# Activations and weight rings of the feed-forward stages placed above 128 KB of each partition

## The chip, the cores and the metric

The kernel runs as one program on one core of a Trainium2 chip. The measure is the time that the device takes for one execution, in microseconds (us), as the median of several runs. TensorE (PE) multiplies matrices and loads the stationary operand (PEld); VectorE (DVE), ScalarE (ACT) and GpSimd (POOL) do elementwise work; SyncE (SP) issues the DMA transfers of weights. Operands lie in SBUF, which has 128 partitions; an address here is the place of a tile within its partition, in KB from its start, and a tile has the same place in each.

## What is computed

A model of two blocks on 256 tokens of width 1024, in float32. The first block (attention, memory attention and a mixture of experts) takes the first 1187 us of the profiled span. The change lies in the second block:

```python
def swiglu(h, w_in, w_out):
    gate, up = jnp.split(h @ w_in, 2, axis=-1)
...
    for l in range(DEPTH):                      # DEPTH = 2
        h = rms_norm(x, norm_ffa[l])
        x = x + 0.5 * swiglu(h, ffa_w_in[l], ffa_w_out[l])
...
        x = x + hybrid_mixer(h, w_in[l], ...)
        h = rms_norm(x, norm_ffb[l])
        x = x + 0.5 * swiglu(h, ffb_w_in[l], ffb_w_out[l])
    return rms_norm(x, norm_final)
```

So there are four feed-forward stages, called here FFN a and FFN b of layers 0 and 1, and a mixer between a and b of each layer. The hidden width of a feed-forward is 2816.

## The kernel before

A float32 operand is split into two float32r parts, hi and lo, and `mm3` (L93) adds three products: hi by hi, lo by hi and hi by lo. A product is one matmul of 128x256 with a weight load of 128 columns.

A feed-forward (`ffn`, L345) runs over 11 chunks of 256 hidden columns. Each chunk has 48 gate products, 48 up products (both against the normed input) and 48 down products (against the activations), 1584 for the stage. The weights of each are one [128, 8, 256] block, which `chunk` (L213) loads in two halves of 512 KB: half i goes through ring i of `e.rings`, a list of three pools each. The load lands in tile `w`; ACT casts it into `whi` (L229); DVE takes the difference into `wlo` (L231). Before, ring 0 is `e.w2`, which lives through the whole block and is the mixers' only ring, and ring 1 (`fw`, `fwhl`, `fwlo`) is opened by `scopes` for the feed-forward.

The normed input is written by `gain_h` (L301): for each of eight row tiles ACT writes `hh` (L308) and DVE `hl` (L309). The sum of squares for the norm is taken beside it (L283 on ACT, two TENSOR_REDUCEs of L284 on DVE, a RECIPROCAL, L290, after a square root on ACT, L289) and applied to the products. `split_act` writes the activations' parts `ah` and `al` (L316, L317) for the down products. A mixer ends with the products of `y` (tiles `y4`) by `w_out`, whose results are added into `xT` (L1031); the next `hh` is read from there.

A scheduler lays out each engine's instructions in one order, in which the engine then works through them; a tile whose place is still read by earlier work can only be written when that work is done. Places follow from the order in which pools are opened. The tiles of the built programs lie as follows (KB; "mod" is the address by 512 bytes):

```
                          before                    after
hh, hl                    26.9, 34.9  mod 416       FFN a l0: 136.2, 144.2  mod 224
                                                    FFN b l0, FFN a l1: 135.2, 143.2  mod 224
                                                    FFN b l1: 135.4, 143.4  mod 416
                                                    mixers: 58.9, 66.9  mod 416
ah, al                    106.9 to 114.9  mod 416   127.2 to 136.2  mod 224
w2 ring (w / whi / wlo)   42.9 / 54.9 / 66.9        26.9 / 38.9 / 50.9  mod 416 both
ring 1 before             74.9 / 86.9 / 94.9        -
ring fa, FFN a l0         -                         81.2 / 93.2 / 105.2  mod 224
rings fa, fb, later       -                         151.2 to 215.4  mod 224 (FFN b l1: mod 416)
first chunk's weights     192.0 to 208.0  mod 480   the same (FFN a l0 only)
y4 of the mixers          129.7 to 165.7  mod 224   the same
block 1: P, nhl (L1790)   172 to 181, 192 to 207, equal mod 512
block 1: hh, weights      208, 130 to 144, differing by 64 mod 512
```

Of the kernel before, what the change touches and what calls it, by code (L numbers as in the profile page):

```python
# [11 lines left out]
F32 = mybir.dt.float32  # L12
# [8 lines left out]
T = 256  # L21
D = 1024
# [19 lines left out]
def constant_tables():  # L42
    """Tables that follow from the shapes alone, laid out by partition."""
# [51 lines left out]
def mm3(nc, out, L, R, first, last, skip=False):  # L95
    """out += L^T R for float32 operands held as two float32r parts each."""
# [7 lines left out]
def bc(ap, axis, n):  # L104
    """Insert a broadcast axis of size n at position axis."""
    shape = list(ap.shape)
    idx = [slice(None)] * axis + [None] + [slice(None)] * (len(shape) - axis)
    shape.insert(axis, n)
    return ap[tuple(idx)].to_broadcast(shape)
# [37 lines left out]
def constants2(e):  # L147
    """The loads of the mixers' constants, and what follows from them."""
# [16 lines left out]
def scopes(e, kind):  # L165
    e.stack = ExitStack()
    P = lambda n, b: e.stack.enter_context(e.tc.tile_pool(name=n, bufs=b, reuse_waits="tile"))
    if kind == "ffn":
        banks(e, bank=4, sbank=2, ubank=2)
        e.rings = [e.w2, [P("fw", 3), P("fwhl", 2), P("fwlo", 3)]]  # L170
        e.act = P("fact", 2)
        e.s1 = P("fs1", 6)
        e.s2 = P("fs2", 4)
        e.s4 = P("fs4", 2)
    elif kind == "mix":
        banks(e, bank=3, abank=3, sbank=2)
        e.rings = [e.w2]
        e.act = P("act", 2)
# [12 lines left out]

def banks(e, **n):
    """The scope's PSUM banks, by ring."""
# [10 lines left out]
def hcol(e, l, name, i):  # L204
    """Half of the vector: a sigmoid is 0.5 tanh(x / 2) + 0.5."""
# [4 lines left out]
def ccol(e, l, name, i):  # L210
    """1 less the vector, or less its half."""
# [4 lines left out]
def chunk(e, src, after=()):  # L216
    """A [128, a, 2048 / a] block of weights; (hi, lo) float32r parts of each of its a row tiles. The lo queue
    behind after."""
# [19 lines left out]
def behind(e, tail):  # L238
    """A block whose instructions are queued behind those of tail, each on its engine."""
# [14 lines left out]
def proj_T(e, u, h, c0=0, bank=None):  # L254
    """One bank [feature, 2, token]: columns c0.. of the chunk's row tiles against h."""
# [9 lines left out]
def proj_N(e, u, h):  # L265
    """One bank [token, 2, column]."""
# [9 lines left out]
def rms_row(e, cols=False, bank=None):  # L276
    """1 / rms of each token, on every partition; with cols also by token on the partitions."""
# [23 lines left out]
def gain_h(e, l, name):  # L301
    """x^T times the norm's gain, split in two parts; 1 / rms is applied to the products."""
    nc = e.nc
    hh = e.per.tile([128, KD, T], F32R, name="hh")
    hl = e.per.tile([128, KD, T], F32R, name="hl")
# [15 lines left out]
def warm(e, fn, after):  # L321
    """Loads an activation's table, behind after."""
# [4 lines left out]
def ffn(e, l, name, wi, wo):  # L327
    nc = e.nc
    if name == "norm_ffa" and l == 0 or name == "norm_ffb":
        scopes(e, "ffn")  # L330
# [16 lines left out]
    for c in range(nc2):  # L347
        u, e.first = e.first, None
# [28 lines left out]
def rope(e, x, cos, sin, half):  # L377
    """In-place rotation of the first 2*half entries of the last axis; x [128, 2, heads, dim]."""
# [1734 lines left out]
```

## Time and profile before

| | |
|---|---|
| three runs | 2719.51, 2721.08, 2724.07 us; median 2721.08 us |
| span of the profiled execution | 2723.9 us, 2.8 us above that median |
| PE busy | 2623.9 us, 96% |
| DVE, ACT busy | 1371.4 us (50%), 1011.8 us (37%) |
| DMA | mean 254 GB/s over the span |

The profile is of one execution; its busy times are those of records on each engine. In the span, FFN a of layer 0 runs from about 1187 to 1380 us, the mixer to 1764, FFN b to 1950; layer 1's FFN a to 2143, its mixer to 2522, its FFN b to 2716.

### The profile page before, as it was taken

To read this page: it belongs to the slowest core of one execution; us is meant where nothing else is said; L and a number is where in the kernel's file an instruction comes from. 1 tells how busy PE (TensorE), PEld (TensorE's weight loads), DVE (VectorE), ACT (ScalarE), POOL (GpSimd) and SP (SyncE) were. 2 spreads that over 40 slices of the span, in tenths; PEclk is the share of its full clock that TensorE was granted. 3 is DMA by queue.
4 is the path that set the end of the run, shared out by engine and by line. 5 is a ranking of instruction groups with operands and counts; after the bars stand their busy time and mean duration, and the time that the engine had idled before them with its cause. 6 is when DMAs were issued, how large, how long until landed. Compare 5 with 4: busy or idle time off the path is not lost.

```text
span 2723.9 us, 43485 instructions
## 1 busy us (share of the span) xinstructions
PE 2623.9 (96%) x17866; PEld 1993.2 (73%) x17866; DVE 1371.4 (50%) x2204; ACT 1011.8 (37%) x1662; POOL 107.1 (4%) x171
## 2 busy tenths in 40 slices
PE   8999998999999998999999999999999999999998
PEld 8643332448543333369999988999999999889998
DVE  6521100027421000055577887765755678977655
ACT  7311000027211000044466554544444565645543
POOL 0000000000000000000000031000000000320000
PEclk9999999999999999999999999999999999999999
DMA  9899999996899999985655533656566555426653
GB/s 348 317 372 409 409 409 377 406 379 218 321 358 409 409 409 384 409 281 180 186 155 153 161 102 101 213 179 186 178 184 182 154 165 157 132 86 189 194 178 116
DMA packets 353715, 691.64 MB, mean 254 GB/s; under 512 B 25872, under 2 KB 229648, under 8 KB 352992
## 3 DMA queue, kind: packets, MB, share of 16 engines
q1 hardware_dynamic: 351488, 681.38, 71.4%
q0 software_dynamic: 976, 5.70, 0.5%
q8 instruction: 145, 2.38, 0.4%
q10 hardware_dynamic: 1040, 1.64, 0.2%
q14 instruction: 66, 0.54, 0.1%
HBM read 684.47 MB, written 4.19 MB: 253 GB/s over the span
## 4 chain that ended last, share of the span: by engine, by line
PE 50%; DMA 5%; DVE 5%; ACT 1%; issue 1%; SPq 0%; DVEq 0%; ACTq 0%
PE sbank L100 23%; PE ubank L100 9%; PE bank L100 9%; PE bank L1843 2%; DVE wlo L231 2%; DMA w<-in_w_up_dram 1%; PE abank L100 1%; DVE t L796 1%; DMA w<-in_w_down_dram 1%; DMA w<-in_w_gate_dram 1%; DMA w<-in_ffb_w_in_dram 1%; PE bank L899 1%; ACT whi L229 0%; DMA w<-in_w_out_dram 0%; DVE t L797 0%
## 5 line engine op out<-in xcount | busy, mean ns | idle before, releaser
L229 ACT CAST whi<-w 128x1024 fp32r<-128x1024 f32 x452 | 471.1, 1049 | 538.5 <-PE sbank L100 249.8
L231 DVE TENSOR_TENSOR wlo<-w,whi 128x1024 fp32r<-128x1024 f32 x452 | 550.3, 1222 | 126.4 <-PE sbank L100 51.7
L1843 PE MATMUL bank<-w,xg 128*64 128x512 f32 x1960 | 492.6, 598 | 24.6 <-DMA w<-in_w_up_dram 21.4
L1843 PEld LDWEIGHTS bank<-w,xg 128*64 128x64 f32 x1960 | 163.7, 136 | 340.3 <-issue 262.3
L100 PE MATMUL sbank<-hh,whi 128*128 128x256 f32 x1408 | 404.8, 288 | 6.5 <-ACT whi L316 6.0
L100 PE MATMUL sbank<-hh,wlo 128*128 128x256 f32 x1408 | 404.0, 287 | 6.1 <-DVE wlo L231 6.0
L100 PE MATMUL sbank<-hl,whi 128*128 128x256 f32 x1408 | 402.6, 286 | 1.0 <-DVE hl L309 0.9
L100 PEld LDWEIGHTS sbank<-hh,whi 128*128 128x128 f32 x1408 | 271.3, 193 | 10.2 <-ACT whi L316 6.6
L100 PEld LDWEIGHTS sbank<-hh,wlo 128*128 128x128 f32 x1408 | 270.9, 193 | 10.2 <-DVE wlo L231 7.0
L100 PEld LDWEIGHTS sbank<-hl,whi 128*128 128x128 f32 x1408 | 271.1, 193 | 4.2 <-issue 2.2
L1843 PE MATMUL bank<-w,aT 128*64 128x512 f32 x1024 | 249.6, 604 | 18.8 <-PEq L1936 12.7
L1843 PEld LDWEIGHTS bank<-w,aT 128*64 128x64 f32 x1024 | 86.3, 138 | 169.1 <-issue 147.9
L100 PE MATMUL ubank<-hh,wlo 128*128 128x256 f32 x704 | 199.4, 283 | 0.0
L100 PE MATMUL ubank<-hh,whi 128*128 128x256 f32 x704 | 199.3, 283 | 0.0
L100 PE MATMUL ubank<-hl,whi 128*128 128x256 f32 x704 | 199.2, 283 | 0.0
L100 PE MATMUL bank<-al,whi 128*128 128x256 f32 x704 | 194.1, 283 | 1.0 <-DVE al L317 1.0
L100 PE MATMUL bank<-ah,wlo 128*128 128x256 f32 x704 | 194.3, 283 | 0.0
L100 PE MATMUL sbank<-wlo,hh 128*128 128x256 f32 x624 | 181.6, 291 | 1.4 <-DVE wlo L231 0.7
L100 PE MATMUL bank<-ah,whi 128*128 128x256 f32 x704 | 179.0, 283 | 0.2 <-ACT ah L316 0.2
L100 PE MATMUL sbank<-whi,hh 128*128 128x256 f32 x624 | 178.4, 287 | 0.0
L100 PE MATMUL sbank<-whi,hl 128*128 128x256 f32 x624 | 178.2, 286 | 0.0
L1910 DVE TENSOR_TENSOR xn<-fbank,xn 128x512 f32<-128x512 f32 x60 | 41.5, 691 | 261.6 <-PE fbank L1908 261.6
(510 smaller groups left out, 4233.6 us busy)
## 6 DMA issues: line engine op xcount, KB each, us to landing
w<-in_w_gate_dram SPq DMA_DIRECT2D x128, 1024.0 KB, 18.4
w<-in_w_down_dram SPq DMA_DIRECT2D x124, 1024.0 KB, 18.4
w<-in_w_up_dram SPq DMA_DIRECT2D x117, 1024.0 KB, 18.4
w<-in_w_in_dram SPq DMA_DIRECT2D x140, 512.0 KB, 3.7
w<-in_ffa_w_in_dram SPq DMA_DIRECT2D x88, 512.0 KB, 4.7
w<-in_ffb_w_in_dram SPq DMA_DIRECT2D x88, 512.0 KB, 4.6
w<-in_ffa_w_out_dram SPq DMA_DIRECT2D x44, 512.0 KB, 4.2
w<-in_ffb_w_out_dram SPq DMA_DIRECT2D x44, 512.0 KB, 4.2
```

The source lines that it names most:

```text
L100: m = nc.tensor.matmul(out, a, b, start=first and i == 0, stop=last and i == 2, skip_group_check=skip)
L229: c = nc.scalar.copy(hi, w)
L231: m = nc.vector.tensor_sub(lo, w, hi.bitcast(F32))
L796: nc.vector.tensor_mul(tmp, X[:, :, :t + 1], bc(LXv[:, :t + 1, t], 1, 16))
L899: nc.tensor.matmul(py[t][32 * c:32 * c + 32, P], RpT[t][:, P, 32 * c:32 * c + 32], cur[:, P], start=True, stop=True, tile_position=(0, 32 ...
L1843: m = nc.tensor.matmul(pb[n][64 * i:64 * i + 64], lhs(k, i), ws[i][j][:, sl], start=k == 0, stop=k == KD - 1, tile_position=(0, 64 * i))
L1910: nc.vector.tensor_add(yacc[t][:, sl], out, yacc[t][:, sl])
```

## The change

`scopes` opens the pools of a feed-forward in another order. In FFN a of layer 0 (where `e.first` is set) the rings stay low, and 15 KB of empty room put the activations and `hh`, `hl` above 128 KB. In the other feed-forwards 46 KB (layer 0) or 34 KB (layer 1) of empty room stand below the activations, `hh`, `hl`, and two rings, `fa` and `fb`, and chunk 0 still takes its first halves through `w2`; from chunk 1 on both halves go through `fa` and `fb`. The mixers get a pool for `hh`, `hl` of their own. Elsewhere the file only loses its docstrings, so line numbers are shifted by up to 20 (L231 is L249, L309 is L327).

```diff
-def scopes(e, kind):
+def scopes(e, kind, l=0):
...
         banks(e, bank=4, sbank=2, ubank=2)
-        e.rings = [e.w2, [P("fw", 3), P("fwhl", 2), P("fwlo", 3)]]
-        e.act = P("fact", 2)
         e.s1 = P("fs1", 6)
         e.s2 = P("fs2", 4)
         e.s4 = P("fs4", 2)
+        ring = lambda n, h=3: [P("w" + n, 3), P("h" + n, h), P("l" + n, 5 - h)]
+        if e.first:
+            a = ring("fa")
+            space(P, 15)
+            e.act = P("fact", 2)
+            e.hp = P("hp", 1)
+            e.steady = [e.w2, a]
+        else:
+            space(P, 46 - 12 * l)
+            e.act = P("fact", 2)
+            e.hp = P("hp", 1)
+            a = ring("fa")
+            e.steady = [a, ring("fb", 2)]
+        e.rings = [e.w2, a]
     elif kind == "mix":
         banks(e, bank=3, abank=3, sbank=2)
         e.rings = [e.w2]
+        e.hp = P("hp", 1)
...
+def space(P, kb):
+
+    P("space", 1).tile([128, 256 * kb], F32, name="space")
...
-    hh = e.per.tile([128, KD, T], F32R, name="hh")
-    hl = e.per.tile([128, KD, T], F32R, name="hl")
+    hh = e.hp.tile([128, KD, T], F32R, name="hh")
+    hl = e.hp.tile([128, KD, T], F32R, name="hl")
...
-        scopes(e, "ffn")
+        scopes(e, "ffn", l)
...
     for c in range(nc2):
+        if c == 1:
+            e.rings = e.steady
...
-    yo = [e.act.tile([128, D], F32, name="yo", bufs=2) for _ in range(2)]
-    z = [e.act.tile([128, 512], F32, name="z", bufs=2) for _ in range(2)]
+    yo = [e.s1.tile([128, D], F32, name="yo", bufs=2) for _ in range(2)]
+    z = [e.s1.tile([128, 512], F32, name="z", bufs=2) for _ in range(2)]
```

The scheduler's order moves with it. On DVE, at the end of layer 0's mixer and the start of FFN b, the program before has these rows (xT of L1031 are the mixer's last additions; wlo of L231 stand for weights of the mixer, then of FFN b; four of the eight hl stand ahead of them):

```order
L1031 TENSOR_TENSOR xT<-sbank,xT 128x512
L231 TENSOR_TENSOR wlo<-w,whi 128x1024 [waits DMAHW2_49,Activation_49]
L231 TENSOR_TENSOR wlo<-w,whi 128x1024 [waits DVE_49,DMAHW4_49,PE_49,Activation_49]
L309 SCALAR_TENSOR_TENSOR hl<-xT,vec,hh 128x256 [waits Activation_49] x2
L231 TENSOR_TENSOR wlo<-w,whi 128x1024 [waits DMAHW5_49,PE_49,Activation_49]
L1031 TENSOR_TENSOR xT<-sbank,xT 128x512
L284 TENSOR_REDUCE t_14650<-t_14652 128x256 [waits Activation_49]
L231 TENSOR_TENSOR wlo<-w,whi 128x1024 [waits DMAHW6_49,DVE_49,PE_49]
L309 SCALAR_TENSOR_TENSOR hl<-xT,vec,hh 128x256 [waits Activation_49] x2
L284 TENSOR_REDUCE t_14651<-t_14655 128x256 [waits Activation_49]
L231 TENSOR_TENSOR wlo<-w,whi 128x1024 [waits DMAHW1_49,PE_49,Activation_49]
L285 TENSOR_TENSOR t_14649<-t_14650,t_14651 128x256 [waits DVE_49]
```

And the changed program these, from the wlo that waits for the mixer's last product on (the second row is the last xT; the wlo are, in turn, those of up's first half, gate's second half, down, up's second half, two of other loads, and after the RECIPROCAL chunk 1's gate):

```order
L249 TENSOR_TENSOR wlo<-w,whi 128x1024 [waits DVE_49,DMAHW7_49,PE_49,Activation_49]
L1051 TENSOR_TENSOR xT<-sbank,xT 128x512
L327 SCALAR_TENSOR_TENSOR hl<-xT,vec,hh 128x256 [waits Activation_49] x8
L302 TENSOR_REDUCE t_14680<-t_14684 128x256 [waits Activation_49]
L249 TENSOR_TENSOR wlo<-w,whi 128x1024 [waits DMAHW2_49,Activation_49,Pool_49]
L249 TENSOR_TENSOR wlo<-w,whi 128x1024 [waits DMAHW0_49,PE_49]
L303 TENSOR_TENSOR t_14678<-t_14679,t_14680 128x256 [waits DVE_49]
L249 TENSOR_TENSOR wlo<-w,whi 128x1024 [waits DMAHW3_49,Activation_49]
L249 TENSOR_TENSOR wlo<-w,whi 128x1024 [waits DMAHW1_49,PE_49,Activation_49]
L249 TENSOR_TENSOR wlo<-w,whi 128x1024 [waits DMAHW4_49,DVE_49,PE_49]
L308 RECIPROCAL t_14690<-t_14690 128x256 [waits Activation_49]
L249 TENSOR_TENSOR wlo<-w,whi 128x1024 [waits DMAHW6_49,DVE_49,PE_49]
```

All eight hl now stand in one piece behind the last xT, the second TENSOR_REDUCE behind them, and the wlo of the chunk's second halves behind that.

On ACT at the same place the program before has (casts of L229 are of weights, hh of L308; four more hh stand ahead):

```order
L229 CAST whi<-w 128x1024 [waits DMAHW1_49]
L229 CAST whi<-w 128x1024 [waits DMAHW2_49,Pool_49]
L229 CAST whi<-w 128x1024 [waits DMAHW4_49,PE_49,Activation_49]
L308 ACTIVATE hh<-xT,vec 128x256 [waits DVE_49]
L308 ACTIVATE hh<-xT,vec 128x256
L229 CAST whi<-w 128x1024 [waits DMAHW5_49,PE_49,Activation_49]
L229 CAST whi<-w 128x1024 [waits DMAHW6_49,PE_49,Activation_49]
L283 ACTIVATE t_14652<-xT 128x1024
L308 ACTIVATE hh<-xT,vec 128x256 [waits DVE_49]
L308 ACTIVATE hh<-xT,vec 128x256
L283 ACTIVATE t_14655<-xT 128x1024
L229 CAST whi<-w 128x1024 [waits DMAHW1_49,PE_49,Activation_49]
```

and the changed program (casts are L247 there, hh is L326), whose second row is the cast that waits for the last but one product of the mixer:

```order
L247 CAST whi<-w 128x1024 [waits DMAHW7_49,DVE_49,PE_49]
L247 CAST whi<-w 128x1024 [waits DMAHW0_49,DVE_49,PE_49]
L326 ACTIVATE hh<-xT,vec 128x256 x4
L326 ACTIVATE hh<-xT,vec 128x256 [waits DVE_49]
L326 ACTIVATE hh<-xT,vec 128x256
L326 ACTIVATE hh<-xT,vec 128x256 [waits DVE_49]
L326 ACTIVATE hh<-xT,vec 128x256
L301 ACTIVATE t_14684<-xT 128x1024
L247 CAST whi<-w 128x1024 [waits DMAHW2_49]
L247 CAST whi<-w 128x1024 [waits DMAHW3_49,Pool_49]
L247 CAST whi<-w 128x1024 [waits DMAHW4_49]
L247 CAST whi<-w 128x1024 [waits DMAHW1_49,PE_49,Activation_49]
```

All eight hh have moved behind the mixer's products.

On DVE at the start of FFN a of layer 0 the program before has, left out between its second and third row some constants and two wlo:

```order
L309 SCALAR_TENSOR_TENSOR hl<-xT,vec,hh 128x256 [waits DMAHW4_49,DMAHW5_49,DMAHW0_49,Activation_49]
L309 SCALAR_TENSOR_TENSOR hl<-xT,vec,hh 128x256 [waits Activation_49] x7
L231 TENSOR_TENSOR wlo<-w,whi 128x1024 [waits DMAHW3_49,Activation_49]
L231 TENSOR_TENSOR wlo<-w,whi 128x1024 [waits DMAHW5_49,Activation_49]
L284 TENSOR_REDUCE t_7741<-t_7743 128x256 [waits Activation_49]
L284 TENSOR_REDUCE t_7742<-t_7746 128x256 [waits Activation_49]
L231 TENSOR_TENSOR wlo<-w,whi 128x1024 [waits DMAHW4_49,DVE_49,PE_49]
L285 TENSOR_TENSOR t_7740<-t_7741,t_7742 128x256 [waits DVE_49]
```

and the changed program, left out in the same way behind the first four rows:

```order
L327 SCALAR_TENSOR_TENSOR hl<-xT,vec,hh 128x256 [waits DMAHW2_49,DMAHW1_49,DMAHW3_49,DMAHW0_49,Activation_49]
L327 SCALAR_TENSOR_TENSOR hl<-xT,vec,hh 128x256 [waits Activation_49] x3
L302 TENSOR_REDUCE t_7748<-t_7750 128x256 [waits DMAHW3_49,DMAHW4_49,DMAHW2_49,Activation_49]
L327 SCALAR_TENSOR_TENSOR hl<-xT,vec,hh 128x256 [waits Activation_49] x4
L249 TENSOR_TENSOR wlo<-w,whi 128x1024 [waits DMAHW5_49,Activation_49]
L249 TENSOR_TENSOR wlo<-w,whi 128x1024 [waits DMAHW4_49,DVE_49,PE_49]
L302 TENSOR_REDUCE t_7749<-t_7753 128x256 [waits Activation_49]
L303 TENSOR_TENSOR t_7747<-t_7748,t_7749 128x256 [waits DVE_49]
L249 TENSOR_TENSOR wlo<-w,whi 128x1024 [waits DMAHW6_49,PE_49]
```

One of the two TENSOR_REDUCEs has moved between the hl, and a wlo that stood behind both now stands ahead of the other.

## Rows read from the trace of the kernel before

**Rows 1.** the page, sections 1 and 2: TensorE's row and its granted clock

```profile
PE 2623.9 (96%) x17866; PEld 1993.2 (73%) x17866; DVE 1371.4 (50%) x2204; ACT 1011.8 (37%) x1662; POOL 107.1 (4%) x171
...
PEclk9999999999999999999999999999999999999999
```

**Rows 2.** windows in the feed-forward: busy us, PEclk, DMA share, GB/s

```profile
1780.00:1950.00 170.00, 169.80 (x1415) 169.60 (x1415) 99.18 (x103) 74.20 (x83) 0.00 (x0) 1.00 0.60 180
1970.00:2140.00 170.00, 170.00 (x1419) 170.00 (x1418) 99.62 (x103) 75.02 (x83) 0.00 (x0) 1.00 0.59 177
```

**Rows 3.** the timeline in FFN b, layer 0, first and last of 28

```profile
1903.78 0.28 PE L100 MATMUL sbank<-hh,wlo 128*128 128x256 f32 x1
...
1907.02 0.28 PE L100 MATMUL ubank<-hl,whi 128*128 128x256 f32 x1
```

**Rows 4.** the timeline in FFN a, layer 0, chunk 0, 28 products

```profile
1194.79 0.28 PE L100 MATMUL sbank<-hh,whi 128*128 128x256 f32 x1
...
1197.97 0.28 PE L100 MATMUL sbank<-hh,whi 128*128 128x256 f32 x1
```

**Rows 5.** the timeline in block 1, first and last of 49

```profile
20.13 0.28 PE L100 MATMUL sbank<-hh,whi 128*128 128x256 f32 x1
...
25.57 0.28 PE L100 MATMUL sbank<-whi,hh 128*128 128x256 f32 x1
```

**Rows 6.** instructions of line 1790: minimum, median, maximum ns

```profile
L1790 PE MATMUL bank<-P,nhl x256: 274/283/775, 112.2 to 922.3; 128*128 128x256 f32 x128
```

**Rows 7.** windows with line 1790 alone, one of six alike

```profile
220.00:223.00 3.00, 2.17 (x16) 1.00 1.02 408
```

**Rows 8.** the timeline of PE at the start of FFN b, layer 0

```profile
1763.83 0.28 PE L100 MATMUL sbank<-hl,whi 128*128 128x256 f32 x1
1764.78 0.39 PE L100 MATMUL sbank<-hh,wlo 128*128 128x256 f32 x1 [0.68 <-DVE wlo L231]
```

**Rows 9.** the same at layer 1

```profile
2521.36 0.28 PE L100 MATMUL sbank<-y,wlo 128*128 128x256 f32 x1
2521.96 0.39 PE L100 MATMUL sbank<-hh,whi 128*128 128x256 f32 x1 [0.33 <-ACT whi L229]
...
2523.22 0.38 PE L100 MATMUL sbank<-hh,wlo 128*128 128x256 f32 x1 [0.76 <-DVE wlo L231]
```

**Rows 10.** the page, sections 5 and 6: casts, subtractions, two loads

```profile
L229 ACT CAST whi<-w 128x1024 fp32r<-128x1024 f32 x452 | 471.1, 1049 | 538.5 <-PE sbank L100 249.8
L231 DVE TENSOR_TENSOR wlo<-w,whi 128x1024 fp32r<-128x1024 f32 x452 | 550.3, 1222 | 126.4 <-PE sbank L100 51.7
...
w<-in_w_in_dram SPq DMA_DIRECT2D x140, 512.0 KB, 3.7
...
w<-in_ffb_w_in_dram SPq DMA_DIRECT2D x88, 512.0 KB, 4.6
```

**Rows 11.** groups of ACT in FFN b, layer 0: busy us, mean ns

```profile
L308 ACT ACTIVATE hh<-xT,vec 128x256 fp32r<-128x256 f32 x3 | 1.4, 500 | 0.0
L289 ACT ACT_TABLE_LOAD x1 | 1.3, 1283 | 0.0
```

**Rows 12.** groups of DVE in FFN b, layer 0

```profile
L284 DVE TENSOR_REDUCE t<-t 128x256 f32<-128x1024 f32 x2 | 4.0, 2024 | 0.0
L290 DVE RECIPROCAL t<-t 128x256 f32<-128x256 f32 x1 | 1.8, 1754 | 0.6 <-ACT t L289 0.6
L309 DVE SCALAR_TENSOR_TENSOR hl<-xT,vec,hh 128x256 fp32r<-128x256 f32 x4 | 1.7, 479 | 0.0
L1031 DVE TENSOR_TENSOR xT<-sbank,xT 128x512 f32<-128x512 f32 x1 | 0.7, 687 | 0.0
```

**Rows 13.** a window at the end of the mixer, layer 0

```profile
1740.00:1763.00 23.00, 22.65 (x191) 22.45 (x191) 17.75 (x21) 12.06 (x16) 0.00 (x0) 1.00 0.76 253
```

**Rows 14.** PE's wait at the mixer's end, layer 0

```profile
1741.17 0.38 PE L100 MATMUL sbank<-y,wlo 128*128 128x256 f32 x1 [0.35 <-DVE wlo L231]
```

**Rows 15.** PE's wait early in FFN a, layer 0

```profile
1205.84 0.39 PE L100 MATMUL sbank<-hh,wlo 128*128 128x256 f32 x1 [1.36 <-DVE wlo L231]
```

## The prediction

> **What bounds it now.** The page comes first: TensorE (PE) is busy 96% of the span and its granted clock stands at nine tenths or more, its higher level of 2.4 GHz, in all 40 slices [rows 1]. Then the windows over the feed-forward stages: PE is busy for the whole of each stretch, 169.80 of 170 us and 170.00 of 170 us, while DVE has 99 us, ACT 74 to 75 us and the DMA share is 0.6 [rows 2]. So in there nothing waits for another engine: time is the number of products times their distance from start to start. That distance is the first thing to read, in the timeline. In FFN b of layer 0 it is 3.24 us for 27 products, 120.0 ns [rows 3]; in the first chunk of FFN a of layer 0, the same 128x256 products, 3.18 us for 27, 117.8 ns [rows 4]; in block 1, 5.44 us for 48, 113.3 ns [rows 5]. Shape, type and clock are alike; where the operands lie is not, as the table of addresses in the kernel's description shows: below 128 KB both (120.0), activations below and weights above (117.8), both above (113.3). The second thing to read is what PE waits for at the seams between mixer and feed-forward, since the change rearranges those.
>
> **The pitch.** The four stages have 4 x 1584 = 6336 products. If a place above 128 KB by itself gave one of the shorter distances, they would gain 6336 x 2.2 ns = 13.9 us at 117.8, and at 113.3 for the three stages that get both operands high (4752 x 6.7 ns = 31.8 us) plus 117.8 for the first (1584 x 2.2 = 3.5 us) 35.3 us.
>
> But the trace has a case that speaks against height. Line 1790 in block 1 multiplies P (172 to 181 KB) by nhl (192 to 207 KB), both above 128 KB, in groups of 16 of the same shape: median length 283 ns [rows 6], and a group takes 2.17 us [rows 7], so (2.17 - 0.28) / 15 = 126 ns a product, no faster than the low ones. What these share with the low products of the feed-forward is the distance of their two addresses: taken by 512 bytes it is 0 (every low tile starts at a remainder of 416, so all their pairs differ by 0). The fast pairs differ by 448 [rows 4] and by 64 [rows 5]. So I take the remainder, not the height, as what decides: 0 gives 120, 64 or 320 or 448 gives 117.8 or less. In the changed kernel the products at 0 stay at 0 nearly everywhere, because a tile moved by whole rows of its ring keeps its remainder: FFN b of layer 0 and FFN a of layer 1 have 0 throughout, FFN b of layer 1 has 0 in its gate and up products. Only 832 products of FFN a of layer 0 (those against the w2 ring) and 528 down products of FFN b of layer 1 come to a distance of 320. That is 1360 x 2.2 ns = **3.0 us gained**. From below nothing (the feed-forward locks to 120 whatever it is), from above 35.3 us.
>
> The Trainium skill goes further: SBUF — State Buffer, in its section on the two separate sides, says that PE never waits on anyone for SBUF, and it names no cost of an address within the partition. By it the term is 0 and the sum below 3.0 us higher; the three distances in the rows speak against it.
>
> **Seam from mixer to FFN b, twice.** T is the start of the mixer's last product. Before, hh lies at 27 KB, where nothing of the mixer is in the way, and six of eight hl were queued on DVE ahead of the last xT; PE lost 0.95 - 0.12 = 0.8 us at layer 0 [rows 8] and 1.86 - 0.36 = 1.5 us at layer 1 [rows 9]. After, hh at 135 KB lies on y4, which the last products still read, so all eight hh and hl stand behind the end. On ACT a cast stands first, then hh: 1.05 us [rows 10] from T + 0.2, then 0.5 us [rows 11], so PE's first product starts at T + 1.75. On DVE a wlo stands first that waits for the last product: 1.22 us [rows 10] from T + 0.35, the last xT 0.69 us, then the first hl 0.48 us [rows 12]. Neighbours on an engine overlap by some 0.09 us, so it ends near T + 2.6, and PE's second product waits until then. Loss: 1.65 + 0.65 = **2.3 us** each.
>
> What is late next: the eight hl, 0.40 us apart, hold DVE until T + 5.4, the second TENSOR_REDUCE (2.02 us) until T + 7.6. Behind it stand the wlo of the gate's second half (to T + 8.8), one for down, an addition, and the one of up's second half (to T + 11.4). PE has 48 products on first halves, 5.8 us, and meets the first of these about on time. But the ring fa now holds three tiles for gate, up and down second halves, so the first half of chunk 1's gate is loaded into the slot that the wlo at T + 8.8 frees. A load lands after 4.6 us in the median [rows 10], 3.7 for the quicker kind, which I take: T + 12.5; its cast, T + 13.6; the ACT table load, 1.28 us [rows 11], and the square root, estimated as an hh of the same shape, T + 15.3; the RECIPROCAL on DVE, 1.75 us [rows 12], T + 17.1; only then this chunk's wlo, T + 18.3. PE, after 96 products and the norm's small one, wants chunk 1 at T + 14.7. Up's cast (load after T + 11.4) holds it to T + 16.3, 1.6 us, the gate's wlo then another 1.7 us: **3.3 us** each. From below 1 us (the loads quicker, other products in between), from above 4.3 us (a landing of 4.6).
>
> **Mixer's end, twice.** Three loads of ring fb are issued there ahead of the last output products, and their three wlo, 3.4 us, come into a stretch in which DVE is already busy 17.75 of 23 us [rows 13]. Today one wait of 0.35 us costs 0.5 us there [rows 14]. I put two waits of 0.9 to 1.0 us in its place: **1.4 us** more each; from below 0, if DVE's 5 idle us take them, from above 3.4 less 0.5.
>
> **FFN a of layer 0.** A wait of 1.36 us for a wlo behind two TENSOR_REDUCEs [rows 15] goes, since one of them moves ahead. It now stands between the fourth and fifth hl, where PE waits some 0.6 us, and the casts and wlo that are then bunched make the first down's al late by 2.0 us, the last chunk 0.4 us: **1.7 us** more in sum; bounds -1.4 and +3. Between FFN b and the next FFN a another 0.5 us. Moving yo and z is after the last product's work and costs nothing; hh's own pool adds no instruction.
>
> **Sum.** 2 x 2.3 + 2 x 3.3 + 2 x 1.4 + 1.7 + 0.5 = 16.2, less the 2.3 us that PE loses today at the two seams: 13.9 us, with bounds of 4 and 22. Less 3.0 us for the pitch: **+10.9 us**. The profiled execution's span, 2723.9 us, would become 2734.8; it is 2.8 us above the median of the runs, 2721.08, to which the same difference gives **2732.0 us**.
>
> **Rivals.**
> - Height decides, at 117.8: 13.9 - 13.9 = 0, about 2721 us. For it: [rows 4] and every low pair at 120. Against it: [rows 6, 7].
> - Height decides, and both operands high give 113.3: 13.9 - 35.3 = -21.4, about 2700 us, the other side. It is one mechanism, the pitch in the three later feed-forward stages; it decides from 13.9 us on, 2.2 ns a product. For it stands [rows 5], against it [rows 6, 7] again.
> - The change moves the place but not the pitch, and the seams cost little (4 us: hl and the loads hidden by products that PE can take first): 4 - 3 = +1, 2722 us. Against it: the queues on DVE and ACT are in order, and the rows under the change show nothing that PE could take.
> - No address matters at all, as the skill's page has it: +13.9, 2735 us.
>
> **Chances.** The forecast 0.47, its own range 2726 to 2740 (seams of 8 to 22, pitch 3). Height at 117.8: 0.17. Height at 113.3: 0.14. Small seams: 0.14. No effect of address: 0.08. A change of 0.2%, 5.4 us, is about what a measurement can tell from none. Faster takes the 0.14, 0.05 of the 117.8 case and 0.03 of others: 0.22. Same takes 0.08 of the 117.8 case, 0.11 of the small seams and 0.07 of the forecast: 0.26. Slower is the rest, 0.52. The range runs from 2708, which leaves out most of the 113.3 case, to 2740.
>
> **What would show it.** Pitch: windows inside FFN b of layer 0 and FFN a of layer 1 again with about 1419 products in 170 us and a product's length of 283 ns; 1440 or more would mean height. FFN a of layer 0 should mix 120 and 118. Seams: PE's first two products of each FFN b start 1.7 and 0.6 us late, and a second pair of waits, for whi and wlo, stands some 15 us after T. Mixer's end: two waits for wlo instead of one. If these waits are there and the pitch is 118 or less all through, the step on remainders was wrong; if the pitch holds and the time doesn't rise, the steps on the seams were.

## The result, and the profile after

The changed kernel takes 2738.79 us in the median of four runs (2738.07 to 2741.92), the kernel before 2721.56 us in four runs beside it (2719.51 to 2724.07). The ratio is 1.0064, with a 95% interval of 1.005 to 1.0079: slower by 17.2 us, where 10.9 us were forecast. The time lies 1.2 us below the upper edge of the stated range, 2740 us.

The page of the changed kernel, TensorE's row and its clock:

```profile
PE 2623.3 (96%) x17866; PEld 1991.4 (73%) x17866; DVE 1370.5 (50%) x2204; ACT 1012.3 (37%) x1662; POOL 106.8 (4%) x171
...
PEclk9999999999999999999999999999999999999999
```

Against [rows 1] the work is the same and PE's busy time too; the span has grown from 2723.9 to 2737.3 us. So PE waits more, or works slower in a few places that the page is too coarse to show.

**Pitch** (the distance of the products from start to start). Windows inside FFN a and FFN b of layer 0, FFN a and FFN b of layer 1 (columns as in [rows 2]):

```profile
1300.00:1370.00 70.00, 70.00 (x603) 70.00 (x603) 40.84 (x42) 31.37 (x35) 0.00 (x0) 1.00 0.59 177
1785.00:1950.00 165.00, 165.00 (x1379) 165.00 (x1378) 91.93 (x94) 67.58 (x74) 0.00 (x0) 1.00 0.59 180
1970.00:2140.00 170.00, 170.00 (x1418) 169.95 (x1417) 102.00 (x106) 74.76 (x82) 0.00 (x0) 1.00 0.57 176
2560.00:2700.00 140.00, 140.00 (x1178) 140.00 (x1177) 77.49 (x80) 57.90 (x64) 0.00 (x0) 1.00 0.60 181
```

A window counts the products that hang over its edges, each 0.28 us long, so the pitch is (length + 0.28) / count: 116.6, 119.9, 120.1 and 119.1 ns. The two stages with everything above 128 KB at remainder 0 keep the 120.0 of [rows 2]. Only the two with some products at a remainder of 320 are quicker. In the trace, product by product, those stand at 114 and 118 ns. With the addresses of the built program beside each product, these are 768 in FFN a of layer 0, not the 832 of the prediction, and the 528 down products of FFN b of layer 1; and FFN b of layer 0 isn't at 0 throughout, since 72 products of its chunk 0 go against the w2 ring at 320.

**Seams.** The timeline of PE from the end of layer 0's mixer to the start of FFN b, the rows with a wait of 0.4 us or more and two others:

```profile
1731.63 0.39 PE L100 MATMUL sbank<-y,wlo 128*128 128x256 f32 x1 [1.36 <-DVE wlo L249]
...
1741.56 0.39 PE L100 MATMUL sbank<-y,whi 128*128 128x256 f32 x1 [0.70 <-ACT y L1046]
1742.63 0.39 PE L100 MATMUL sbank<-y,wlo 128*128 128x256 f32 x1 [0.69 <-DVE wlo L249]
...
1762.05 0.28 PE L100 MATMUL sbank<-y,wlo 128*128 128x256 f32 x1
1763.76 0.39 PE L100 MATMUL sbank<-hh,whi 128*128 128x256 f32 x1 [1.43 <-ACT hh L326]
...
1764.70 0.39 PE L100 MATMUL sbank<-hl,whi 128*128 128x256 f32 x1 [0.43 <-DVE hl L327]
...
1765.44 0.42 PE L100 MATMUL sbank<-hh,whi 128*128 128x256 f32 x1
...
1780.49 0.39 PE L100 MATMUL ubank<-hh,whi 128*128 128x256 f32 x1 [2.16 <-ACT whi L247]
```

At the mixer's end the single wait of [rows 14] has become two for wlo, and one of 0.70 us for a y between them. The mixer's last product starts at 1762.05 (T): hh comes at T + 1.71, hl at T + 2.65, forecast were T + 1.75 and T + 2.6. Chunk 1 is held until T + 18.4 by a cast. What that cast waited for stands in ACT's timeline:

```profile
1776.02 1.28 ACT L307 ACT_TABLE_LOAD   x1
1777.31 0.47 ACT L307 ACTIVATE t<-ubank,eps 128x256 f32<-128x256 f32 x1
1779.39 1.04 ACT L247 CAST whi<-w 128x1024 fp32r<-128x1024 f32 x1 [1.61 <-DMA w<-in_ffb_w_in_dram]
```

ACT was idle for 1.61 us before it: the load is late, not ACT. By the built program it is the load of up's first half, and SyncE issued it here, as soon as the wlo that frees its slot was done:

```profile
1773.38 0.37 SPq L244 DMA_DIRECT2D w<-in_ffb_w_in_dram  x1
```

From there to the cast it takes 6.0 us, where the prediction put 3.7. So far this is the forecast's picture. But the row at 1765.44 shows what it did not have: a product of 0.42 us instead of 0.28, with no wait. Windows on that stretch and on the one behind it:

```profile
1765.30:1768.60 3.30, 3.30 (x18) 3.30 (x17) 3.24 (x7) 3.30 (x7) 0.00 (x0) 0.50 1.08 380
...
1769.00:1774.50 5.50, 5.50 (x48) 5.50 (x47) 5.47 (x6) 3.49 (x4) 0.00 (x0) 1.00 0.66 182
```

The granted clock is 0.50 in the first, the lower level of 1.2 GHz, and 1.00 in the second. Such a stretch is called a fall in what follows. Behind the two waits at the start of FFN b PE runs 15 products at 213 ns each, start to start, and loses 1.43 us that no column of waits shows, since PE counts as busy. The same stands at 1956.5 (16 products behind a wait of 1.51 us for an ah at FFN b's end) and at 2548.3 (10 products): 3.9 us together, at places where the trace of before has no such stretch. The Trainium skill (TensorE: Matmul & The Clock Gate, section on the back-to-back issue gap) gives N ÷ 1.2 GHz for the gap of single matmuls at the lower clock, by which an estimate for 256 columns is 213 ns; the trace agrees. For the higher clock it gives N ÷ 2.4 GHz + 2.5 ns, by the same estimate 109 ns; no run here has 20 float32r products of 128x256 in a row with a mean under 113.2.

**FFN a of layer 0**, PE's waits at its start and at its first down products:

```profile
1193.74 0.39 PE L100 MATMUL sbank<-hl,whi 128*128 128x256 f32 x1 [0.93 <-DVE hl L327]
...
1197.92 0.39 PE L100 MATMUL sbank<-hl,whi 128*128 128x256 f32 x1 [0.84 <-DVE hl L327]
...
1220.76 0.39 PE L100 MATMUL bank<-al,whi 128*128 128x256 f32 x1 [1.84 <-DVE al L335]
```

The wait of [rows 15] is gone; a wait between hl, of 0.84 us where 0.6 was forecast, and one for al, 1.84 us where 2.0 was, stand in its place. A second execution of both kernels (below) shows which of these waits belong to the change.

### The profile page after: what moved, and what is told of

It is laid out like the page before. It is cut to its first block, busy times and chain, and to the rows that moved or that the text cites. A ratio compares the mean times of both kernels' runs of the same rounds, so it can differ in the third digit from the quotient of the medians.

```text
span 2737.3 us, 43490 instructions
## 1 busy us (share of the span) xinstructions
PE 2623.3 (96%) x17866; PEld 1991.4 (73%) x17866; DVE 1370.5 (50%) x2204; ACT 1012.3 (37%) x1662; POOL 106.8 (4%) x171
## 4 chain that ended last, share of the span: by engine, by line
PE 48%; DMA 5%; DVE 5%; ACT 1%; issue 1%; SPq 0%; DVEq 0%; ACTq 0%
PE sbank L100 23%; PE bank L100 9%; PE ubank L100 9%; DVE wlo L249 2%; DMA w<-in_w_up_dram 1%; PE abank L100 1%; PE bank L1863 1%; DMA w<-in_w_gate_dram 1%; DVE t L816 1%; DMA w<-in_ffb_w_in_dram 1%; DMA w<-in_w_down_dram 1%; PE bank L919 1%; DVE t L817 0%; ACT whi L247 0%; PE bank L925 0%
## 5 line engine op out<-in xcount | busy, mean ns | idle before, releaser
L247 ACT CAST whi<-w 128x1024 fp32r<-128x1024 f32 x452 | 471.3, 1050 | 541.4 <-PE sbank L100 266.2
L249 DVE TENSOR_TENSOR wlo<-w,whi 128x1024 fp32r<-128x1024 f32 x452 | 551.0, 1222 | 190.0 <-PE sbank L100 86.7
## 6 DMA issues: line engine op xcount, KB each, us to landing
w<-in_w_gate_dram SPq DMA_DIRECT2D x128, 1024.0 KB, 18.4
w<-in_w_down_dram SPq DMA_DIRECT2D x124, 1024.0 KB, 18.3
w<-in_w_up_dram SPq DMA_DIRECT2D x117, 1024.0 KB, 18.4
```

The costliest lines, as they stand in the source:

```text
L247: c = nc.scalar.copy(hi, w)
L249: m = nc.vector.tensor_sub(lo, w, hi.bitcast(F32))
```

## The experiments

Two theories of the pitch: *remainder* (the distance of the two operands' addresses, taken by 512 bytes, decides) and *height* (a place above 128 KB decides). Two of the seams: that hh and hl on y4's place make the loss, or that ring fb's early loads do. In what follows d is the remainder.

**Pitch 1: the kernel before with two pads of 64 bytes, nothing moved above 128 KB.**

```diff
+    e.padded = False
...
+        P("apad", 1).tile([128, 16], F32, name="apad")
         e.act = P("fact", 2)
...
     hl = e.per.tile([128, KD, T], F32R, name="hl")
+    if not e.padded:
+        e.per.tile([128, 16], F32, name="pad")
+        e.padded = True
```

> The kernel before with nothing moved above 128 KB: only 64 bytes of room are put ahead of the weight rings and another 64 ahead of the activations, so that every 128x256 product of the feed-forward and of the mixers' projections has its two operands 64 or 448 bytes apart, taken by 512, instead of 0. If the remainder decides the distance between products, windows inside all four feed-forwards show 113 to 118 ns instead of 120.0, and some 9,600 products gain 2.2 to 6.1 ns each: 20 to 58 us, so 2663 to 2700 us. If the height decides, nothing changes: 120 ns and 2721 us.

Measured: 2699.2 us, ratio 0.9917 (0.9901 to 0.9934). Windows in FFN a and FFN b of layer 0:

```profile
1240.00:1360.00 120.00, 120.00 (x1031) 120.00 (x1030) 70.67 (x74) 52.74 (x59) 0.00 (x0) 1.00 0.61 188
1800.00:1930.00 130.00, 130.00 (x1117) 130.00 (x1116) 76.14 (x78) 56.50 (x62) 0.00 (x0) 1.00 0.61 190
```

That is 116.7 and 116.6 ns instead of 120.0, and 116.8 and 116.7 in layer 1, with everything where it was but for 64 and 128 bytes. Nothing had to lie high for that: *remainder* holds. Whether height adds something is for Pitch 2.

**Pitch 2: the changed kernel with pads, everything left as high as the change put it**, d now 448 or 64 for the products that stood at 0 (448 and 192 in the last stage).

```diff
         if e.first:
+            P("padx", 1).tile([128, 16], F32, name="padx")
             a = ring("fa")
             space(P, 15)
+            P("pady", 1).tile([128, 16], F32, name="pady")
...
+            if l:
+                P("padw", 1).tile([128, 16], F32, name="padw")
             e.hp = P("hp", 1)
+            P("padz", 1).tile([128, 16], F32, name="padz")
             a = ring("fa")
```

> The changed kernel, with 64 bytes of room ahead of its rings (twice in FFN a of layer 0, where one lies ahead of the activations, and in layer 1 once more ahead of hh), so that the operands lie high as before and nearly all differ by 64, 192 or 448 bytes. The waits at the seams stay. By the remainder some 4,900 products of the three later feed-forwards and the half of FFN a of layer 0 that ran at 120 gain 2.2 to 6.1 ns: 11 to 30 us, 2709 to 2728 us. If height adds something to the remainder, the distance in here is shorter than in the low kernel with the same remainders; if it doesn't, the two are alike.

Measured: 2709.12 us, ratio to before 0.9954 (0.9938 to 0.9969). Windows in the first and the last feed-forward:

```profile
1240.00:1360.00 120.00, 120.00 (x1061) 120.00 (x1061) 72.98 (x76) 55.10 (x60) 0.00 (x0) 1.00 0.64 196
...
2560.00:2670.00 110.00, 110.00 (x971) 109.92 (x970) 67.12 (x69) 50.03 (x55) 0.00 (x0) 1.00 0.61 192
```

113.4 and 113.6 ns; the two between stand at 117.4 and 117.7. The same two distances come up high as low, and no third one. Which of the two a stage takes isn't fixed by d: with 448 throughout, the two stages between stand at 117.4 and 117.7 here, and low down (Pitch 4) three of four stand at 113. Whether height has a part in this choice is open. The seams' waits are as in the changed kernel (1.71 and 0.71 us from start to start at FFN b, then 2.18), and with them this kernel is 9.9 us behind Pitch 1 although its pitch is better in two stages.

**Pitch 3: other remainders at low places**, pads as in Pitch 1, but 128 bytes behind hl (hh at 384) and 32, 192 or 256 bytes ahead of the activations, by stage.

```diff
-def scopes(e, kind):
+def scopes(e, kind, pad=64):
...
+        P("apad", 1).tile([128, pad // 4], F32, name="apad")
...
+        e.per.tile([128, 32], F32, name="pad")
...
-        scopes(e, "ffn")
+        scopes(e, "ffn", 32 if name == "norm_ffa" else 192 if l == 0 else 256)
```

> The kernel before with other remainders: the normed input 384 bytes from the weights (128 where the weights move), the activations 32 in FFN a of layer 0, 192 in FFN b of layer 0 and FFN a of layer 1, 256 in FFN b of layer 1. By the remainder: odd multiples of 64 are fast, so 192 gives 113 to 118 ns; 128 and 256 stay near 119 to 120, as the few products at 256 in the changed kernel did; 32 is open. By height: 120 everywhere.

One run: 2707.71 us. Windows in FFN a of layer 0 and in FFN b of layer 1:

```profile
1230.00:1370.00 140.00, 140.00 (x1189) 140.00 (x1188) 80.65 (x82) 59.70 (x66) 0.00 (x0) 1.00 0.58 180
...
2530.00:2670.00 140.00, 140.00 (x1181) 140.00 (x1180) 79.67 (x81) 59.65 (x65) 0.00 (x0) 1.00 0.59 184
```

118.0 and 118.8 ns. Product by product, d = 384 stands at 118.6, 256 at 119.1, 32 at 117.0, 192 at 116.0, the last two as a mix of values from 113 to 120. Even multiples of 64 gain little; odd ones give 113 or 118 where all products of a stage stand at odd ones.

**Pitch 4 and 5: the pad ahead of the activations of Pitch 1 at 448 bytes (112 floats) and at 192 (48 floats)**, the one behind hl still 64.

```diff
+        P("apad", 1).tile([128, 48], F32, name="apad")
```

> The kernel before with 64 bytes of room ahead of the rings and 448 ahead of the activations: all products of hh and of the activations stand 448 bytes apart, nothing is moved above 128 KB. In the low kernel with 448 and 64 the products of the activations always ran at 118 ns and those of hh at 113 or 118 in runs of 22 or 24. If the remainder alone picks between 113 and 118, the activations now run as hh does; if a state carries over from one operand to the next, hh keeps 113 for longer as well, and the mean falls from 116.5 towards 114: 2683 to 2699 us.

> The same with 192 bytes ahead of the activations: 448 for hh, 192 for the activations, the pair that ran at 113.4 throughout FFN b of layer 1 in the high kernel. If that pair holds 113.4 by its remainders, all feed-forwards do so here, low as they lie: 2680 to 2688 us. If it was height, or where the state happened to fall, the mean stays near 116: 2695 to 2702 us.

Measured: 2688.5 us, ratio 0.9865 (0.9842 to 0.9888), and 2684.37 us, ratio 0.9853 (0.9837 to 0.987). Windows of the second in the four feed-forwards (the first has the same four counts):

```profile
1250.00:1350.00 100.00, 100.00 (x885) 100.00 (x884) 59.01 (x61) 43.90 (x48) 0.00 (x0) 1.00 0.64 195
1800.00:1920.00 120.00, 120.00 (x1021) 120.00 (x1020) 68.75 (x70) 51.24 (x56) 0.00 (x0) 1.00 0.60 187
1975.00:2100.00 125.00, 125.00 (x1106) 125.00 (x1105) 76.32 (x79) 56.62 (x62) 0.00 (x0) 1.00 0.62 193
2540.00:2660.00 120.00, 120.00 (x1061) 120.00 (x1061) 71.42 (x74) 54.42 (x60) 0.00 (x0) 1.00 0.60 184
```

113.3, 117.8, 113.3 and 113.4 ns. The second version, the kernel before plus 256 bytes of room, is faster than the kernel before by 1.5% and than the changed one by 2.0%: what the change looked for is to be had without moving anything up. The time came as expected, but not that all feed-forwards hold 113.4: FFN b of layer 0 stands at 117.8 with the same remainders as the others. So at odd multiples of 64 there are two states; which of them a stage falls into is open.

**Seam 1: the changed kernel without ring fb** (chunks from 1 on use w2 and fa).

```diff
-            e.steady = [a, ring("fb", 2)]
+            e.steady = [e.w2, a]
```

> The changed kernel without ring fb: in all feed-forwards first halves go through the w2 ring and second halves through fa, which stays at 151 KB on the mixer's y4. If the three loads of fb make the waits at the mixer's end (1.6, 1.0 and 1.1 us in layer 0), these go back to the one of 0.6 us of before, and if the three second halves in a row through fa make the wait of 2.4 us for chunk 1, it goes too; the wait for hh of 1.7 and 0.7 us at the start stays. By the remainder the first halves' products then stand 320 bytes apart and run at 113 to 118 ns, some 2 to 5 us less per stage. Sum: 2714 to 2726 us. If fa's place on y4 is what makes the waits of chunk 0 and 1, they stay: 2722 to 2732 us.

Measured: 2715.88 us, ratio to before 0.997 (0.9961 to 0.998). The waits of PE from 1724 to 1785 us (sum, times, longest):

```profile
PE sbank L100 <- ACT hh L326: 1.4, 1, 1.4
PE sbank L100 <- DVE hl L327: 0.8, 1, 0.8
PE sbank L100 <- DVE wlo L249: 0.3, 1, 0.3
PE ubank L100 <- DVE wlo L249: 0.2, 1, 0.2
```

The waits at the mixer's end are back at the one of [rows 14], and chunk 1 no longer waits for a cast. Both came with ring fb (in chunk 1 the first halves, which came through fa when fb took the second ones, now come through w2); those for hh and hl did not. Of the 22.9 us between the two medians (25.6 by the two ratios, since the kernel before ran at 2723.24 us beside this one) some 9.3 are pitch: half of the products of FFN b of layer 0 and FFN a of layer 1 now meet w2 at d = 320 and stand at 114, so the two stages average 117.0 and 116.9 ns (2.9 and 3.1 ns less, 1584 products each). The rest are waits and what hangs on them.

**Seam 2: every feed-forward laid out as FFN a of layer 0** (rings low, only activations, hh and hl high).

```diff
-        if e.first:
+        if True:
```

> The changed kernel with all feed-forwards laid out as its FFN a of layer 0: rings low, only activations, hh and hl above 128 KB, hh still on y4. The waits for hh and hl at the start of each FFN b (1.7 and 0.7 us) stay, since they come from hh's place; the waits at the mixer's end and for chunk 1 go, since they come from the rings. About half of the products stand 320 or 192 bytes apart and gain 2 to 6 ns: 2 to 5 us per stage. Sum about 2706 to 2718 us. If hh's place alone makes all the waits, they are all there still: 2715 to 2725 us.

Measured: 2717.33 us, ratio to before 0.998 (0.997 to 0.999). PE's first product of FFN b, layer 0:

```profile
1762.40 0.39 PE L100 MATMUL sbank<-hh,whi 128*128 128x256 f32 x1 [2.29 <-ACT hh L326]
```

One wait, 2.6 us from start to start (3.6 at layer 1), in place of the three of the changed kernel there; the mixer's end has its one wait of 0.36 us, and chunk 1 none. The time lies in both of the expected ranges, so the waits have to decide. The rings lie low here as in the kernel before, which has no wait for hh at the start of FFN b of layer 0: so the wait for hh comes with the place of hh and hl, and neither ring fa nor fb is needed for it.

**Seam 3: the changed kernel with hh and hl back at 27 and 35 KB**, all remainders 0. Two things move here, not one: without the 16 KB of hh and hl the rings move down with them. In the built program fa of FFN b of layer 0 starts at 135.4 KB instead of 151.2, and fb at 167.4 instead of 183.2, so the expectation's words that they stay are wrong.

```diff
-            space(P, 15)
+            P("padx", 1).tile([128, 48], F32, name="padx")
...
-    hh = e.hp.tile([128, KD, T], F32R, name="hh")
-    hl = e.hp.tile([128, KD, T], F32R, name="hl")
+    hh = e.per.tile([128, KD, T], F32R, name="hh")
+    hl = e.per.tile([128, KD, T], F32R, name="hl")
```

> The changed kernel with hh and hl back at 27 and 35 KB, in their old pool, and room chosen so that all remainders are 0: the rings fa and fb and the activations stay where the change put them. If the place of hh on y4 makes the waits at the start of FFN b, the wait of 1.6 us for hh and 0.6 us for hl there goes back to the 0.8 to 1.5 us of before, and the second TENSOR_REDUCE comes earlier, so that the wait of 2.3 us for chunk 1 shrinks as well; it gains 2 to 9 us by that, and loses 6 us of pitch that the changed kernel has in FFN a of layer 0 and FFN b of layer 1: 2735 to 2743 us. If rings and loads make these waits, they stay, and the time is 2745 us.

Measured: 2738.9 us, ratio to before 1.0063 (1.0046 to 1.008), no different from the changed kernel. The waits of PE from 1764 to 1785 us:

```profile
PE sbank L100 <- ACT whi L247: 7.2, 2, 5.6
PE ubank L100 <- ACT whi L247: 1.0, 1, 1.0
```

The waits for hh and hl are gone, and others stand in their place: 8.2 us for casts of loaded weights. The DMA issues from 1755 to 1785 us show why, with the median time to landing last, here and in the changed kernel:

```profile
w<-in_ffb_w_in_dram SPq DMA_DIRECT2D x10, 512.0 KB, 8.3
...
w<-in_ffb_w_in_dram SPq DMA_DIRECT2D x7, 512.0 KB, 3.7
```

They take 8.3 us, and they come in one bunch. The changed kernel issues five loads of FFN b through ring fb from 1720 us on (the first three lines, of its SyncE); here no load of FFN b is issued before 1753 us (the last):

```profile
1720.30 0.97 SPq L244 DMA_DIRECT2D w<-in_ffb_w_in_dram  x2
1721.32 0.50 SPq L244 DMA_DIRECT2D w<-in_ffb_w_out_dram  x1
...
1728.13 2.10 SPq L244 DMA_DIRECT2D w<-in_ffb_w_in_dram  x2
...
1753.29 3.26 SPq L244 DMA_DIRECT2D w<-in_ffb_w_in_dram  x2
```

In the built program fb now begins inside the mixer's pool of y4 (125.7 to 169.7 KB), and its loads stand behind the mixer with those of fa. So this run confirms that the place of hh and hl makes the waits for them, and it loses at layer 0 as much by late loads as it gains: from the mixer's end to the end of FFN b it takes 239.3 us, the changed kernel 238.3 and 240.5. With no early loads through fb the mixer's end has one wait of 0.35 us again, which fits Seam 1. What the changed kernel's own rings would do with hh and hl low was not run. Of the two theories of the seams, then, neither is enough alone: hh and hl make the first waits, ring fb those at the mixer's end and, with fa, at chunk 1.

**Executions 1 and 2: the changed kernel and the kernel before, unaltered, profiled once more.**

> The changed kernel unaltered, to read a second profiled execution of it. In the first, PE's granted clock is 0.50 for some 15 products of 213 ns (instead of 120) at 1765.4, 1956.5 and 2548.3 us, each behind a wait of PE in the feed-forward; before has no such stretch there. Theory A: each of these falls belongs to its wait and costs some 1.4 us every time: then they stand at the same three places again, FFN a of layer 0 takes 191.6 us again and the two waits there (1.3 and 2.1 us) again bring none. Theory B: whether a wait of 1.3 us or more brings a fall differs from one execution to the next: then the waits are the same to some 0.1 us, and the falls stand elsewhere, behind the first product or the al of FFN a, say, where three other kernels with the same places had them (193.9 us for that stage). Time 2736 to 2742 us by both.

> The kernel before unaltered, a second profiled execution. In the first, the mixer of layer 0 has a wait of 2.5 us ahead of line 842 at 1601 us, with eight products at half clock behind it, and takes 224.6 us from its first product to y where six other kernels with the same mixer take 220.7 to 222.1. If that is of this one execution, as I expect, it is gone here, the stretch takes 220.7 to 222.1 us and the feed-forwards show again no product at 213 ns; if it belongs to the kernel's order, it is there again and the change did take it away. Time 2719 to 2725 us.

One run each: 2740.36 and 2720.40 us (another run of the kernel before beside them took 2725.55). The changed kernel's second execution, PE's wait for chunk 1:

```profile
1780.25 0.58 PE L100 MATMUL ubank<-hh,whi 128*128 128x256 f32 x1 [2.87 <-ACT whi L247]
```

and windows at the mixer's end, behind that wait and at the start of FFN b:

```profile
1742.80:1745.90 3.10, 3.10 (x16) 3.10 (x16) 0.14 (x1) 0.35 (x1) 0.00 (x0) 0.50 0.48 162
1781.40:1783.60 2.20, 2.20 (x12) 2.20 (x12) 1.18 (x2) 1.34 (x3) 0.00 (x0) 0.50 0.75 220
...
1766.00:1774.00 8.00, 8.00 (x69) 7.91 (x68) 7.93 (x11) 6.77 (x9) 0.00 (x0) 1.00 0.79 259
```

At FFN b of layer 0 the waits for hh and hl are the same to 0.01 us, and so are those for al in FFN a and for y at the mixer's end; those for loaded weights (chunk 1, the mixers) and for the first hl of FFN a are not. The clock falls at other places: not at the start of FFN b, but at the mixer's end, behind chunk 1's wait, behind both waits of FFN a, at FFN b's end again and at the start of the last stage: six falls, 8.3 us, where the first execution had three, 3.9 us. So the second theory of this run holds: a wait brings the risk of a fall, and which one pays differs from one execution to the next.

The kernel before, in its second execution, does not have the wait of [rows 15], but this at the start of FFN a, with a fall behind it that was not expected:

```profile
1191.48 0.38 PE L100 MATMUL sbank<-hl,whi 128*128 128x256 f32 x1 [1.73 <-DVE hl L309]
```

```profile
1193.40:1196.20 2.80, 2.80 (x15) 2.80 (x15) 2.80 (x7) 2.80 (x4) 0.00 (x0) 0.50 0.02 6
```

So the wait of [rows 15] belonged to that one execution. The changed kernel's second execution has the same wait for the first hl there, 1.73 us, and none between the hl; its wait for al is 1.84 us again. Only the last is in both executions of the one kernel and in neither of the other. The mixer of layer 0 of the kernel before takes 221.4 us from its first product to its first with y, where the first execution took 224.6, with a fall of its own. The window of that first execution:

```profile
1605.10:1606.70 1.60, 1.60 (x9) 1.60 (x9) 1.60 (x6) 0.43 (x2) 0.00 (x0) 0.50 0.39 84
```

That slow mixer is why the first pair of spans differs by 13.4 us only, less than the medians (17.2); the second pair differs by 20.1 (2738.6 and 2718.5).

## Why the prediction was right, and where its sizes were off

The sign, and the step that remainder and not height decides, held; the time lies inside the range, and the rise of 17.2 us is 6.3 above the forecast. With two executions of each kernel the stages can be set side by side, each from the start of its first product to that of the next stage's (the nth product of PE is the same in both programs), in us:

| stage | before, two executions | after, two executions | difference of the means |
|---|---|---|---|
| FFN a, layer 0 | 194.60, 195.16 | 191.64, 193.98 | -2.1 |
| end of the mixer, layer 0 (288 products) | 34.60, 34.49 | 39.55, 40.88 | +5.7 |
| FFN b, layer 0 | 192.41, 192.55 | 198.79, 199.60 | +6.7 |
| FFN a, layer 1 | 191.36, 191.36 | 190.50, 190.49 | -0.9 |
| end of the mixer, layer 1 | 35.52, 34.82 | 39.70, 38.71 | +4.0 |
| FFN b, layer 1, to the last product | 193.37, 193.37 | 197.36, 196.82 | +3.7 |

The sum is +17.2 us (-2.07 + 5.67 + 6.72 - 0.87 + 4.04 + 3.72), as large as the difference of the medians; the rest of the two pairs of spans, the first block and the mixers up to there, differs by -0.5 us in the mean (-2.3 and +1.4). The prediction's terms, one by one, against the same two pairs of executions:

| term | predicted | first pair, second pair |
|---|---|---|
| pitch | -3.0 | -6.3, -6.6 |
| hh and hl at FFN b, twice | +4.6 | +4.3, +4.4 |
| chunk 1, twice | +6.6 | +5.4, +5.2 |
| mixer's end, twice | +2.8 | +5.1, +4.9 |
| waits of FFN a, layer 0 | +1.7 | +1.7, +2.3 |
| ends of the later feed-forwards | +0.5 | +1.8, +1.8 |
| today's seams, gone | -2.3 | -2.2, -2.2 |
| products at the lower clock | none | +3.9, +7.0 |

The sums are 13.7 and 16.8 us against stage differences of 15.7 and 18.7; what is missing, 2.0 and 1.9 us, lies for the most part in distances of 0.16 to 0.4 us next to the waits, such as the first product behind each (0.22 us).

- **The pitch** was right in its cause (Pitch 1 and 2 show it) and, but for their count, in the products that it touches, but its size was taken from the nearer of the two fast distances. The step "1360 x 2.2 ns" took 117.8 of [rows 4]; the products of FFN a of layer 0 that it means (768 of them, not 832) run at 113.4 to 114.7 in the trace, near the 113.3 of [rows 5], and gain some 6 ns each. FFN b of layer 1 got what was forecast, 118. The reading of line 1790, 126 ns a product from a group's length, was rough: from start to start the median in the trace is 120 ns, and 192 of its 256 products stand at d = 0, the others at 384. That speaks more clearly against height than the 126 did.
- **hh and hl** came as worked out, at layer 0 to 0.05 us. The cause is shown: the wait for hh stays with the rings low (Seam 2), and both are gone with hh and hl low (Seam 3).
- **Chunk 1** is held to T + 18.4 and T + 17.7 at layer 0 and to T + 18.6 and T + 18.7 at layer 1, forecast T + 18.3. At layer 1 it is the gate's wlo that PE waits for last, as worked out. At layer 0 it is up's cast, forecast for T + 16.3: its load, issued at T + 11.3 as forecast, took 6.0 us where 3.7 were put, and the gate's wlo, done at T + 18.6, came without a wait. That the two fell together there is luck. The loss at layer 0 was 2.3 us in the first execution, where PE came later itself by 1.4 us of lower clock, and 3.0 in the second, with no fall there.
- **FFN a of layer 0** came out near its number, but not by its steps. The wait of [rows 15], whose end the prediction put down to the moved TENSOR_REDUCE, is missing in the second execution of the kernel before too, and the wait between the hl in that of the changed kernel. What both executions share is the late al, 2.0 us as forecast, and 0.35 us at the last chunk.
- **The ends of the later feed-forwards** cost 1.8 us where 0.5 was put: 1.3 us for an ah in layer 0's FFN b and 1.0 in layer 1's, less 0.5 us that FFN a of layer 1 no longer waits.
- **Mixer's end** was mis-sized: 2.5 us a layer where 1.4 was put between bounds of 0 and 2.9. Two waits for wlo, of 1.5 and 1.0 us, came as said, and at layer 0 a third for y; the 5 idle us of DVE in [rows 13] hid little of it. Seam 1 shows that it goes with ring fb.
- **The clock** was missing altogether: the prediction took PE's higher level in [rows 1] as given, and priced a wait at its own length. Behind some of its waits (1.43 and 0.43 us close together, for instance, or 2.87 us in one) PE ran at 1.2 GHz, in these two kernels' feed-forwards and mixers' ends for 10 to 16 products of 213 ns, 1.0 to 1.5 us that stand in busy time. That is the largest of the errors, 3.9 and 7.0 us. The loss it adds and the larger gain in the pitch partly cancel, and without that luck the time would have lain above the range.

Height at either distance and the rule that no address matters can't be brought together with 2699 us and 2684 us from pads alone (Pitch 1 and 5). The Trainium skill (SBUF — State Buffer, section on the two separate sides) names no cost of an address within the partition; these runs show one. It doesn't say that there is none, which the prediction reads into it. Small seams, 4 us, fall by the table: the terms of the seams add up to 16.1 and 16.4 us without the clock.

## What to carry to other kernels

Where PE is busy throughout, read the distance from start to start of its products, stage by stage, and compare it with the addresses of the two operands: here 256 bytes of padding gained 1.5%, and a rearrangement over 46 KB of room lost 0.6%. Before a tile is moved onto the place of another, look who reads that place last, since everything written there queues behind it on every engine in between. And price a stall of PE with the clock that it may cost: read the granted clock of the products behind the wait, and take a second execution before a single wait becomes a term.

## What the runs showed of the hardware that was not expected

- Products of 128x256 in float32r follow each other at 120.0 ns when the two operands' addresses are equal by 512 bytes, at 119.1 for a distance of 256, 118.6 for 384, and at 113.3 or 117.8 for odd multiples of 64; both values come up low and high. Between the two there is a state that lasts: the kernel with 448 and 192 holds 113.3 through FFN a of layer 0, 117.8 through FFN b, then 113.3 again. With 448 and 64 (Pitch 1) the distance changed between 113 and 118 in runs of 22 to 24 products, often where gate or up products and down products took turns, which suggests that the operands used just before count. What sets the state was not found.
- The lower clock does not follow every long wait. In the changed kernel's first execution the wait of 2.16 us for chunk 1 and that of 1.84 us for al brought none; in the second both did (2.87 and 1.84 us).
